# A decoder layer on one core: prompt scores from unsplit queries and keys on the two row halves of the array, and four instead of two channel tiles convolved beside the prompt heads

## The chip, the cores and the metric

One core of a Trainium2 chip runs the whole program. The metric is the device time of one execution in microseconds; of several runs the median counts. Engines are named as the profile names them: PE is TensorE (PEld its weight load), DVE is VectorE, ACT is ScalarE, POOL is GpSimd, SP is SyncE, which here issues DMAs only.

## The reference

One inference step of one layer, for a prompt of 512 tokens and a batch of 8 sample tokens (one each, with 2048 tokens of cached past), all in fp32. D is 1024, there are 16 heads of 64 and 4 groups of keys and values.

```python
z = rms_norm(x, ln1_g) @ w_in            # 6704 columns: u (2048), q, six k/v, head gates, two merge gates
u = u2[..., :D_CONV] * sigmoid(u2[..., D_CONV:])
conv_out = silu(layer_norm(depthwise_conv31(u) + conv_b)) @ w_pw
# attention: three branches (compressed, selected, window), each with its own k and v
s = (q * 64 ** -0.5) @ k.T - slope[head] * (t_q - t_k)      # masked: t_k <= t_q
o = softmax(s) @ v
attn_out = g[0] * o_cmp + g[1] * o_sel + g[2] * o_win       # sigmoid gates per head
m = sigmoid(g_conv) * conv_out + sigmoid(g_attn) * attn_out
x = x + m @ w_out
x = x + square(relu(rms_norm(x, ln2_g) @ w_up)) @ w_down    # 4096 wide
y = rms_norm(x, lnf_g)
```

## The kernel before, in words

**Layout.** All activations lie channel-major: a tile holds 128 channels by 520 tokens (512 of the prompt, 8 samples), and eight tiles make the 1024 channels. Every fp32 matrix product with a weight is made of three reduced-precision (fp32r) ones. The weight is cast to fp32r by ACT (`wh`, L411), the rest `raw - wh` is the low half `wl` (L412), and the activation is split in the same way into `hH` and `hL`. `dense()` adds wh·aH, wh·aL and wl·aH for eight tiles of the inner dimension and two halves of the tokens (L433 to L435): 48 matmuls of some 260 columns for each 128 columns of a weight. `wload()` has SP fetch the raw weight in two pieces. POOL makes the low halves (`LOW[0]`), except those of loads 2 to 5 and of the feed-forward, which DVE makes.

**Stages.** The start is the norm (`norm1()`, L325 ff.), in an order that the string `NORDER` writes out: q squares a tile of tokens on ACT, s takes the statistics of tiles a to b (with a Newton step, L218 to L221, on DVE), m scales a tile (L338), t transposes it on PE and splits it. Then follow two stages in which generators take turns by weights (`run()`); the instructions of each are then placed by a scheduler that goes by priorities, and each engine executes its instructions in the order so found.

The first stage (about 57 to 455 us) holds the prompt's heads. `project()` makes q, k and v of a group, `cmp_kv` the compressed keys, `pool_cache()` gathers and pools the samples' cached rows (L783, L790), and `attend(g)` goes through two pairs of heads, each with three branches: selected (r = 0), window (r = 1), compressed (r = -1). For a branch, a head and a tile of 128 queries there is a score matmul (L688) into one of the two banks of `pss`, a reduction with the distance penalty and the maximum on DVE (`score()`, L651) and an exponential on ACT (L655). After that come the weights, transposes on PE (L750), copies to `pt` (L753), and the product with V (L755), for which the two heads take the two column halves of the array. Beside it `u_proj()` projects the convolution's input u of two channel tiles (`U_EARLY` says behind which score), and `conv_taps()` convolves them: 31 operations on DVE for a channel tile, 30 of them L1108.

For L688 a query tile is split in two (`build_q()`): the rows of head e hold the cast query, the other 64 rows its rest. The key is split in `build_k()` and copied by DMA to both row halves. Two matmuls with all 128 rows, against the cast key and against its rest, then give the score. The tiles of both are called `rt`.

The second stage (to about 725 us) holds the samples' attention, 20 units of a gather of 1 MB (`sg`, issued by POOL), transposes (L936), scores (L940), a reduction (L943), an exponential and the product with V. Beside it run the other six channel tiles (u and taps), the gates `gate_attn()` and `gate_conv()`, and, once all tiles are convolved, the convolution's norm and activation (`conv_norm`, `conv_act`, `conv_split`, L1179 to L1226), which make `cH` and `cL`. Then follow the pointwise product with `merge()`, which takes `cH` as its input, the output projection, the feed-forward and the last norm.

The functions that the change touches:

Of the kernel before, what the change touches and what calls it, by code (L numbers as in the profile page):

```python
# [17 lines left out]
P = 128  # L18
# [15 lines left out]
KTS_B, SG_B, U1, Y1, UP1 = 5, 6, 2, 2, 2  # L34
# [6 lines left out]
LOW2 = "gpsimd"  # L41
# [4 lines left out]
RT_E = lambda nc: nc.gpsimd  # L46
# [6 lines left out]
WR_B, RT_B = 3, 5  # L53
# [3 lines left out]
U_EARLY = (32, 48, 0, 0)  # L57
# [73 lines left out]
def hybrid_layer(ctx: ExitStack, tc: tile.TileContext, I, C, O):  # L131
# [141 lines left out]
    def small_loads():  # L273
        nc.sync.dma_start(wp, I["cmp_w"][0])
# [10 lines left out]
        for i, n in enumerate(("ln2_g", "conv_b", "conv_ln_g", "conv_ln_b")):  # L285
            nc.sync.dma_start(vr[8 * i:8 * i + 8], I[n][0].rearrange("(k p) -> k p", p=P))
        nc.sync.dma_start(cwr, I["conv_w"][0])
# [33 lines left out]
    def norm1():  # L321
# [14 lines left out]
        def scale(j):  # L336
            n = P if j < 4 else NB
            dve.scalar_tensor_tensor(xts[j][:n], xts[j][:n], rs[:n, 0, j:j + 1], g1b[:n], op0=OP.mult, op1=OP.mult)  # L338
# [16 lines left out]
        for op in NORDER.split():  # L355
            a = int(op[1])
            if op[0] == "q":
                squares(a)
            elif op[0] == "s":
                stats(slice(a, int(op[2])))  # L360
            elif op[0] == "m":
                scale(a)
            else:
                last = turn(a)
# [15 lines left out]

    hH = hp.tile([P, KD, T], F32R, name="hH", tag="H")
# [22 lines left out]
    def wload(w, pieces, r0=0, low=None):  # L404
# [46 lines left out]
    ckD = plp.tile([P, NKV, 2, 32], F32R, name="ckD")  # L451
# [16 lines left out]
    def cmp_kv(ap):  # L468
# [49 lines left out]
        for s in range(2):  # L518
            for d in range(2):
                act.activation(ckD[64 * d:64 * d + 64, s:4:2, 0], ps[64 * s:64 * s + 64], AF.Copy, scale=0.5)  # L520
                dve.scalar_tensor_tensor(ckD[64 * d:64 * d + 64, s:4:2, 1], ps[64 * s:64 * s + 64], 0.5,
                                         f32(ckD[64 * d:64 * d + 64, s:4:2, 0]), op0=OP.mult, op1=OP.subtract)
# [32 lines left out]
    def project(g):  # L555
# [4 lines left out]
        kv = kt, vtok = t4[:, 2 * T:3 * T], t4[:, 3 * T:].rearrange("p (t r d) -> p t r d", t=4, r=2)  # L560
# [43 lines left out]
    RT, HP, HV = {}, [], []  # L604

    def build_q(g, pr, ap):
        qc = QC[g]
        t = RT[g, "q", pr] = ap.tile([P, 2, NP_ + 32], F32R, name="rt", bufs=RT_B)
        for e in range(2):
            a, o = 64 * e, 64 - 64 * e  # L610
            act.copy(t[a:a + 64, e, :NP_], qc[a:a + 64, pr, :NP_])
            RT_E(nc).tensor_tensor(t[o:o + 64, e, :NP_], qc[a:a + 64, pr, :NP_], f32(t[a:a + 64, e, :NP_]), op=OP.subtract)

    def build_k(g, r, ap):
        kt = KV[g][0]
        w = ap.tile([P, 2, NP_ + 32], F32R, name="rt", bufs=RT_B)
        t = RT[g, "k", r] = w[:, :, 32:]
        RT[g, "ck", r] = w
        if r == 1 and g > 0:
            add_ck(g)  # L620
        a, o = 64 * r, 64 - 64 * r
        act.copy(t[a:a + 64, 0], kt[a:a + 64, :NP_])
        dve.tensor_sub(t[a:a + 64, 1], kt[a:a + 64, :NP_], f32(t[a:a + 64, 0]))
        DUP_E(nc).dma_start(f32(t[o:o + 64]), f32(t[a:a + 64]))

    def add_ck(g):
        act.copy(RT[g, "ck", 1][:, :, :32], f32(ckD[:, g]))

    def attend(g, ap):
        while g not in QC:  # L630
            yield
        if g == 0:
            build_q(0, 0, ap)
            build_k(0, 0, ap)
            build_k(0, 1, ap)
            build_q(0, 1, ap)
            yield
        elif RT_B < 6:
            build_q(g, 1, ap)
# [1004 lines left out]
```

## Time and profile before

| | |
|---|---|
| median of 3 runs | 1199.09 us (1196.57 to 1199.47) |
| profiled execution, its time | 1196.95 us |
| its span | 1195.2 us |
| mean granted PE clock | 0.981 of full speed |
| PE busy | 1126.9 us (94%) |
| DVE busy | 773.2 us (65%) |
| ACT busy | 557.1 us (47%) |
| POOL busy | 385.2 us (32%) |

All rows are of the one profiled execution, whose span lies 1.75 us below the time of the same execution. Busy shares are means over stages with different limits, so they are read by stage. "out<-in" names the tiles that an instruction writes and reads; what stands behind "<-" in square brackets, or in a wait, is what ended the idle time ahead.

### The profile page before, as it was taken

How to read it: one execution, taken by the hardware profiler on the slowest of the kernel's cores; microseconds unless marked ns; L12 is line 12 of the kernel's file. 1: busy time of each engine (PE TensorE's matmuls, PEld its weight loads, DVE VectorE, ACT ScalarE, POOL GpSimd, SP SyncE). 2: the span in 40 equal slices, each digit the busy share in tenths (PEclk: the TensorE clock that was granted, in tenths of full speed). 3: DMA queues.
4: the chain of work that ended last, by engine and by line, in shares of the span. 5: the costliest groups of instructions: out<-in, count | busy, mean ns of one | idle time of the engine just before them, and what ended most of it. 6: DMA issues, size and time to landing. Idle time of an engine off the chain costs nothing.

```text
span 1195.2 us, 24820 instructions
## 1 busy us (share of the span) xinstructions
PE 1126.9 (94%) x9755; PEld 1025.3 (86%) x9755; DVE 773.2 (65%) x1712; ACT 557.1 (47%) x1404; POOL 385.2 (32%) x378
## 2 busy tenths in 40 slices
PE   6899999998999999989889979999999999999996
PEld 6787976876776888878777769999999999999996
DVE  6442566595977868999998886456543443443476
ACT  5453477545667544445444454344431441431454
POOL 2435637545652333545553334440000000000012
PEclk8899999999999999999999889999999999999999
DMA  6645654564468417867774233333333333333354
GB/s 180 196 137 165 191 168 118 158 175 150 116 185 298 133 38 274 279 241 250 252 253 169 64 105 108 89 89 107 89 96 100 89 89 89 95 99 90 89 164 138
DMA packets 189037, 176.78 MB, mean 148 GB/s; under 512 B 35309, under 2 KB 171053, under 8 KB 183656
## 3 DMA queue, kind: packets, MB, share of 16 engines
q1 hardware_dynamic: 172472, 96.54, 28.5%
q0 software_dynamic: 15296, 76.55, 18.2%
q10 hardware_dynamic: 1152, 2.10, 0.8%
q8 instruction: 77, 1.26, 0.4%
q14 instruction: 40, 0.33, 0.1%
HBM read 167.58 MB, written 14.80 MB: 153 GB/s over the span
## 4 chain that ended last, share of the span: by engine, by line
PE 71%; DVE 20%; DMA 4%; issue 2%; SPq 1%; ACT 1%; POOL 1%; DVEq 0%; POOLq 0%; ACTq 0%
PE psd L433 18%; PE psd L435 17%; PE psd L434 17%; DVE y L1108 13%; PE pss L688 4%; PE pst L750 3%; PE pso L755 3%; PE psp L783 2%; DMA wraw<-in_w_in_dram 1%; DMA cg<-in_cache_cmp_kv_dram,gic 1%; DVE tq L943 1%; DVE y L1212 1%; DMA rt<-rt 1%; PE pso L729 1%; PE psp L790 1%
## 5 line engine op out<-in xcount | busy, mean ns | idle before, releaser
L411 ACT CAST wh<-wraw 128x512 fp32r<-128x512 f32 x282 | 161.7, 617 | 266.9 <-PE psd L434 201.8
L433 PE MATMUL psd<-hH,wh 128*128 128x256 f32 (+2 forms) x848 | 248.3, 295 | 2.2 <-ACT gc L1249 1.3
L435 PE MATMUL psd<-hH,wl 128*128 128x256 f32 (+2 forms) x848 | 247.1, 294 | 0.1
L434 PE MATMUL psd<-hL,wh 128*128 128x256 f32 (+2 forms) x848 | 245.7, 291 | 0.0
L412 POOL TENSOR_TENSOR wl<-wraw,wh 128x512 fp32r<-128x512 f32 x130 | 180.7, 1409 | 199.5 <-ACT wh L411 188.3
L1108 DVE SCALAR_TENSOR_TENSOR y<-u,cwT,y 128x512 f32<-128x512 f32 x240 | 221.7, 924 | 6.0
L433 PEld LDWEIGHTS psd<-hH,wh 128*128 128x128 f32 (+1 forms) x848 | 160.7, 190 | 7.6 <-issue 2.5
L435 PEld LDWEIGHTS psd<-hH,wl 128*128 128x128 f32 (+1 forms) x848 | 160.4, 190 | 4.3 <-issue 2.8
L434 PEld LDWEIGHTS psd<-hL,wh 128*128 128x128 f32 (+1 forms) x848 | 160.8, 190 | 1.8 <-issue 0.7
L433 PE MATMUL psd<-xgH,wh 128*128 128x264 f32 (+1 forms) x512 | 144.8, 283 | 0.0
L434 PE MATMUL psd<-aT,wh 128*128 128x264 f32 (+1 forms) x512 | 144.7, 283 | 0.0
L433 PE MATMUL psd<-aT,wh 128*128 128x264 f32 (+1 forms) x512 | 144.7, 283 | 0.0
L435 PE MATMUL psd<-aT,wl 128*128 128x264 f32 (+1 forms) x512 | 144.7, 283 | 0.0
L435 PE MATMUL psd<-xgH,wl 128*128 128x264 f32 (+1 forms) x512 | 144.5, 282 | 0.0
L412 DVE TENSOR_TENSOR wl<-wraw,wh 128x512 fp32r<-128x512 f32 x152 | 103.9, 723 | 62.5 <-ACT wh L411 59.3
L434 PE MATMUL psd<-xgL,wh 128*128 128x264 f32 (+1 forms) x512 | 144.2, 282 | 0.0
L1583 POOL TENSOR_TENSOR attnT<-attnT,gfb 128x512 f32<-128x512 f32 (+1 forms) x8 | 10.5, 1331 | 368.7 <-DVE sqd L1578 368.7
L434 PEld LDWEIGHTS psd<-xgL,wh 128*128 128x128 f32 x512 | 96.6, 189 | 0.0
L655 ACT ACTIVATE pp<-pp,st 128x256 f32<-128x256 f32 (+3 forms) x128 | 71.6, 559 | 53.7 <-DVE st L651 52.1
L435 PEld LDWEIGHTS psd<-xgH,wl 128*128 128x128 f32 x512 | 96.5, 188 | 0.0
L433 PEld LDWEIGHTS psd<-aT,wh 128*128 128x128 f32 x512 | 96.3, 188 | 0.1
L433 PEld LDWEIGHTS psd<-xgH,wh 128*128 128x128 f32 x512 | 96.3, 188 | 0.0
(378 smaller groups left out, 2326.3 us busy)
## 6 DMA issues: line engine op xcount, KB each, us to landing
wraw<-in_w_in_dram SPq DMA_DIRECT2D x88, 256.0 KB
wraw<-in_w_down_dram SPq DMA_DIRECT2D x80, 256.0 KB
wraw<-in_w_up_dram SPq DMA_DIRECT2D x64, 256.0 KB
sg<-in_state_win_kv_dram POOLq DMA_DIRECT2D x8, 1024.0 KB
out_dram<-in_state_win_kv_dram SPq DMA_DIRECT2D x8, 1022.0 KB
wraw<-in_w_in_dram SPq DMA_DIRECT2D x32, 128.0 KB
wraw<-in_w_conv_pw_dram SPq DMA_DIRECT2D x16, 256.0 KB
wraw<-in_w_out_dram SPq DMA_DIRECT2D x16, 256.0 KB
```

What stands on the lines that cost most here:

```text
L411: act.copy(a, raw[:, :, :o])
L412: (low or (dve if 2 <= len(loaded) < LOW_D else LOW[0])).tensor_tensor(b, raw[:, :, :o], f32(a), op=OP.subtract)
L433: pe.matmul(ps[:n], wh[:, k, :n], aH[:, k, c], start=(k == 0), stop=False)
L434: pe.matmul(ps[:n], wh[:, k, :n], aL[:, k, c], start=False, stop=False)
L435: end = pe.matmul(ps[:n], wl[:, k, :n], aH[:, k, c], start=False, stop=(k == KD - 1))
L655: act.activation(ph, ph, AF.Exp, scale=-1.0, bias=st[:, 0, e, i:i + 1], accum_out=st[:, 1, e, i:i + 1])
L688: hpe = pe.matmul(ps, rq[:, e, P * i:P * i + P], kk[:, l, 32 - xi:32 + nk], start=(l == 0), stop=(l == 1))
L729: packed([lambda i=i, e=e: pe.matmul(po[64 * e:64 * e + 64, P * i:P * i + P], VcZ[:, i], pt[:, e], start=False, stop=True, skip_group_chec ...
L750: pe.transpose(ps[:, o:o + P], phs[e][i][:, P * j:P * j + P], ident)
L755: packed([lambda j=j, e=e: pe.matmul(po[64 * e:64 * e + 64, P * j:], vt[:, j, r], pts[e][:, off[j]:off[j] + P * (4 - j)], start=(r == 0 an ...
L783: packed([lambda r=r, j=j, i=i: pe.matmul(po[32 * i:32 * i + 32, j], wpa[:, 2 * rh + r, j], gs[i][:, r, 256 * j:256 * j + 256], start=(rh ...
L1108: prev = dve.scalar_tensor_tensor(yk, u[:, w:w + NP_], cwT[:, k, w:w + 1], yk, op0=OP.mult, op1=OP.add)
```

## The change

Scores are made in fp32 from the unsplit query and key. A head's query lies in one row half of its tile, so its score needs 64 rows. The key is kept for both row halves: one half as projected, the other as a copy in `ks`. The scores of both heads of a pair are issued together (`packed`), in the steps of query tiles (0, 1), (2) and (3), each head in its own bank; a step waits for the last reduction of both heads. The split tiles `rt` go. The memory lets four channel tiles instead of two have their u and y in the first stage. Low halves from the second stage on are made by DVE, the last two loads and products of the convolution's gate wait for the last sample score, and the start has another order of its norm and of its small loads. The size of a DMA scratch area is now given, 16384.

```diff
-KTS_B, SG_B, U1, Y1, UP1 = 5, 6, 2, 2, 2
+KTS_B, SG_B, U1, Y1, UP1 = 5, 6, 2, 4, 4
-LOW2 = "gpsimd"
+LOW2 = "vector"
-U_EARLY = (32, 48, 0, 0)
+U_EARLY = (32, 48, 56, 74)
-NORDER = "q0 s01 q1 m0 s12 m1 t0 t1 q2 q4 q3 s25 m4 m2 t4 m3 t2 t3"
+NORDER = "q0 q1 s02 m0 m1 t0 t1 q2 q4 q3 s25 m4 m2 t4 m3 t2 t3"
+HELD = 6
     def small_loads():
+        nc.sync.dma_start(cwr, I["conv_w"][0])
+        for i, n in enumerate(("ln2_g", "conv_b", "conv_ln_g", "conv_ln_b")):
+            nc.sync.dma_start(vr[8 * i:8 * i + 8], I[n][0].rearrange("(k p) -> k p", p=P))
...
-    def wload(w, pieces, r0=0, low=None):
+    def wload(w, pieces, r0=0, low=None, ins=None):
...
-            (low or (dve if 2 <= len(loaded) < LOW_D else LOW[0])).tensor_tensor(b, raw[:, :, :o], f32(a), op=OP.subtract)
+            with after(ins):
+                (low or (dve if 2 <= len(loaded) < LOW_D else LOW[0])).tensor_tensor(b, raw[:, :, :o], f32(a), op=OP.subtract)
...
-    ready = [wload(w_in, [(C_Q + P * t, P)]) for t in range(2)]
+    ready = [wload(w_in, [(C_Q + P * t, P)], ins=scaled[1]) for t in range(2)]
...
-    def build_q(g, pr, ap):
...
-    def build_k(g, r, ap):
+    def build_k(g, ap):
+        kw = KV[g][0]
+        ks = ap.tile([P, 32 + NP_], F32, name="ks", bufs=2)
         for e in range(2):
...
+            a, o = slice(64 * e, 64 * e + 64), slice(64 - 64 * e, 128 - 64 * e)
+            KR[g, e, e], KR[g, e, 1 - e] = kw[a], ks[a]
+            if g > 0:
+                DUP_E(nc).dma_start(ks[a, 32:], kw[o, 32:32 + NP_])
+            else:
+                (act.copy if e else dve.tensor_copy)(ks[a, 32:], kw[o, 32:32 + NP_])
...
+            rq = lambda e, i: QC[g][64 * e:64 * e + 64, pr, P * i:P * i + P]
...
-                            for l in range(2):
-                                hpe = pe.matmul(ps, rq[:, e, P * i:P * i + P], kk[:, l, 32 - xi:32 + nk], start=(l == 0),
-                                                stop=(l == 1))
...
+                    for step in ((0, 1), (2,), (3,)):
+                        pb = [pss([P, 512]) for e in range(2)]
...
+                                mms.append(lambda ps=ps, e=e, i=i, xi=xi, nk=nk: pe.matmul(
+                                    ps, rq(e, i), KR[g, e, r][:, 32 - xi:32 + nk], start=True, stop=True))
...
+                        hpe = packed(mms, *last_read.values())
...
     def gate_conv():
         for k in range(KD):
+            while k >= HELD and "scored" not in UY:
+                yield
...
+            dense(wh, wl, hH, hL, lambda hf, c, ps: act.activation(gc[:, c], ps, AF.Tanh, scale=0.5),
+                  ins=UY["scored"] if k >= HELD else None)
```

In the code of the change the lines stand a few lower: L414 is the low half, L679 the score, L739 the transposes, L744 the product with V, L934 the reduction of a sample unit, L1099 the tap.

PE in the middle of the prompt heads, before: scores (L688) stand alone, one head and query tile at a time, among dense matmuls and the pooling of cached rows.

```order
L434 MATMUL psd<-hL,wh 128x264
L688 MATMUL pss<-rt 128x384 x2
L688 MATMUL pss<-rt 128x256 x2
L783 MATMUL psp<-cg,wpa 32x256 x16
L433 MATMUL psd<-hH,wh 128x256
L434 MATMUL psd<-hL,wh 128x256
L435 MATMUL psd<-hH,wl 128x256
L433 MATMUL psd<-hH,wh 128x256
L434 MATMUL psd<-hL,wh 128x256
L688 MATMUL pss<-rt 128x512 x2
```

And now, at a place among the prompt heads:

```order
L744 MATMUL pso<-pt,qkv 64x128 x2
L739 MATMUL pst<-ident,pp 128x128 x3
L679 MATMUL pss<-qkv 128x384
L679 MATMUL pss<-ks,qkv 128x384
L791 MATMUL psp<-pl,w1bd 128x256
L739 MATMUL pst<-ident,pp 128x128 x3
L744 MATMUL pso<-pt,qkv 64x512 x2
L739 MATMUL pst<-ident,pp 128x128 x3
L679 MATMUL pss<-qkv 128x512
L679 MATMUL pss<-ks,qkv 128x512
```

A query tile's scores are now two single matmuls side by side, one from the projected keys (in `qkv`) and one from the copy `ks`. Over the whole stage, PE has 1542 dense matmuls of the input projection ahead of the first sample matmul (its input is `KX`) before, and 1795 in the changed kernel.

DVE near the end of the samples' attention, before (`tq` and `sst` are a unit's biased scores and maximum, `cacc` the sum over channels): the taps go on until the last units, and the norm of the convolution (L1179 ff.) follows them.

```order
L1108 SCALAR_TENSOR_TENSOR y<-u,cwT,y 128x512 x9
L943 ISA tq,sst<-psy,bm 128x512
L943 ISA sst 128x1
L1108 SCALAR_TENSOR_TENSOR y<-u,cwT,y 128x512 x2
L963 COPY a_8136<-sst 32x16 x4
L1080 TENSOR_TENSOR cacc<-cacc,y 128x512
L943 ISA tq,sst<-psy,bm 128x512
L943 ISA sst 128x1
L963 COPY a_8136<-sst 32x16 x4
L1179 TENSOR_TENSOR y<-y,u 128x520 x2
```

And now, where the taps end:

```order
L1099 SCALAR_TENSOR_TENSOR y<-u,cwT,y 128x512 x5
L414 TENSOR_TENSOR wl<-wraw,wh 128x512 x2
L1099 SCALAR_TENSOR_TENSOR y<-u,cwT,y 128x512
L1071 TENSOR_TENSOR cacc<-cacc,y 128x512
L934 ISA tq,sst<-psy,bm 128x512
L934 ISA sst 128x1
L1170 TENSOR_TENSOR y<-y,u 128x520 x8
L414 TENSOR_TENSOR wl<-wraw,wh 128x512 x2
L934 ISA tq,sst<-psy,bm 128x512
L934 ISA sst 128x1
```

Eight of the 20 units' reductions still follow, and the norm's operations now lie between them, with the low halves (L414), which were POOL's. After the heads DVE has 180 taps before and 120 now, and 31 low halves ahead of merge, where it had none.

## Rows read from the trace of the kernel before

**Rows 1.** Stages: columns us, PE, PEld, DVE, ACT, POOL busy (x), PEclk, DMA share, GB/s.

```profile
75.00:450.00 375.00, 361.36 (x2978) 295.76 (x2977) 248.00 (x755) 211.78 (x655) 189.36 (x206) 1.00 0.53 157
450.00:725.00 275.00, 244.94 (x2489) 215.58 (x2489) 249.99 (x392) 133.33 (x290) 117.73 (x103) 0.96 0.60 206
725.00:1195.00 470.00, 460.16 (x3843) 459.14 (x3842) 239.65 (x464) 177.48 (x382) 53.58 (x38) 0.99 0.34 102
```

**Rows 2.** The page's chain that ended last, by engine and by line.

```profile
PE 71%; DVE 20%; DMA 4%; issue 2%; SPq 1%; ACT 1%; POOL 1%; DVEq 0%; POOLq 0%; ACTq 0%
PE psd L433 18%; PE psd L435 17%; PE psd L434 17%; DVE y L1108 13%; PE pss L688 4%; PE pst L750 3%; PE pso L755 3%; PE psp L783 2%; DMA wraw<-in_w_in_dram 1%; DMA cg<-in_cache_cmp_kv_dram,gic 1%; DVE tq L943 1%; DVE y L1212 1%; DMA rt<-rt 1%; PE pso L729 1%; PE psp L790 1%
```

**Rows 3.** Narrower stretches, columns as in rows 1.

```profile
450.00:475.00 25.00, 25.00 (x240) 22.72 (x239) 20.21 (x28) 9.97 (x21) 6.06 (x7) 1.00 0.82 315
450.00:650.00 200.00, 181.41 (x1931) 159.02 (x1931) 190.96 (x258) 95.26 (x216) 96.66 (x88) 0.98 0.73 255
550.00:575.00 25.00, 20.64 (x214) 18.98 (x215) 24.47 (x34) 13.09 (x30) 11.52 (x10) 0.95 0.78 275
700.00:725.00 25.00, 16.70 (x124) 16.20 (x124) 20.90 (x31) 13.26 (x23) 5.59 (x5) 0.86 0.22 64
950.00:975.00 25.00, 25.00 (x211) 25.00 (x210) 12.81 (x26) 12.13 (x28) 0.00 (x0) 1.00 0.29 85
```

**Rows 4.** DVE's timeline at the start; PE's waits from 0 to 75 us.

```profile
7.81 1.28 DVE L338 SCALAR_TENSOR_TENSOR xt<-xt,rs,g1b 128x1024 f32<-128x1024 f32 x1 [0.76 <-DMA g1b<-in_ln_g_dram]
...
9.83 1.03 DVE L218 TENSOR_TENSOR rs<-rs 128x1 f32<-128x1 f32 x1
...
13.34 2.25 DVE L338 SCALAR_TENSOR_TENSOR xt<-xt,rs,g1b 128x1024 f32<-128x1024 f32 x1
...
22.34 0.16 DVE L218 TENSOR_TENSOR rs<-rs 128x3 f32<-128x3 f32 x1
...
PE pss L346 <- DVE xt L338: 5.6, 2, 5.4
...
PE pst L308 <- DMA cwr<-in_conv_w_dram: 2.6, 1, 2.6
```

**Rows 5.** The chain in order of time, 60 to 75 and 100 to 116 us.

```profile
64.91 0.47 PE pss L688 x2
...
103.78 1.01 PE pso L755 x4
...
108.47 0.80 PE pso L755 x4
...
112.36 0.80 PE pso L755 x8
...
113.73 1.06 PE psp L790 x4
```

**Rows 6.** Groups by line and shape, 0 to 460 us, on POOL and DVE.

```profile
L612 POOL TENSOR_TENSOR rt<-qkv,rt 64x512 fp32r<-64x512 f32 x16 | 21.9, 1369 | 29.2 <-DMA cg<-in_cache_cmp_kv_dram,gic 12.0 <-ACT rt L611 7.1 <-DMA bd<-in_cache_cmp_kv_dram,gib 5.2
...
L651 DVE CUSTOM_DVE_ANT_0 pp<-pss,dist 128x512 f32<-128x512 f32 x32 | 22.0, 686 | 11.7 <-PE pss L688 6.2 <-issue 3.0 <-PE pss L697 2.1
```

**Rows 7.** Groups by line, taps from 450 to 725 us, DVE's low halves in the page.

```profile
L1108 DVE SCALAR_TENSOR_TENSOR y<-u,cwT,y 128x512 f32<-128x512 f32 x179 | 165.6, 925 | 5.0
...
L412 DVE TENSOR_TENSOR wl<-wraw,wh 128x512 fp32r<-128x512 f32 x152 | 103.9, 723 | 62.5 <-ACT wh L411 59.3
```

**Rows 8.** Timelines of DVE and of POOL, 470 to 493 us.

```profile
476.44 6.80 DVE L1108 SCALAR_TENSOR_TENSOR y<-u,cwT,y 128x512 f32<-128x512 f32 x5
...
489.60 3.89 DVE L1108 SCALAR_TENSOR_TENSOR y<-u,cwT,y 128x512 f32<-128x512 f32 x5
...
475.31 3.45 POOL L412 TENSOR_TENSOR wl<-wraw,wh 128x512 fp32r<-128x512 f32 x2 [10.73 <-PE psy L940]
```

**Rows 9.** Waits from 450 to 725 us: us in total, times, longest.

```profile
POOL wl L412 <- ACT wh L411: 82.9, 16, 18.6
...
PE psd L433 <- ACT cH L1225: 6.6, 1, 6.6
```

More of the change, by code (lines that the diff above doesn't have):

```diff
@@ L450, in hybrid_layer @@
     pool.memset(gbh, 0.0)
-    ckD = plp.tile([P, NKV, 2, 32], F32R, name="ckD")
+    ckD = plp.tile([P, NKV, 32], F32, name="ckD")
     VcD = plp.tile([P, NKV, HD], F32, name="VcD")
@@ L601, in project @@
             yield
[L604 to L608 removed]
+    KR, HP, HV, last_read = {}, [], [], {}
+    def build_k(g, ap):
+        kw = KV[g][0]
+        ks = ap.tile([P, 32 + NP_], F32, name="ks", bufs=2)
         for e in range(2):
[L610 to L619 removed]
+            a, o = slice(64 * e, 64 * e + 64), slice(64 - 64 * e, 128 - 64 * e)
[4 more added lines that the diff above has]
+                (act.copy if e else dve.tensor_copy)(ks[a, 32:], kw[o, 32:32 + NP_])
+        if g > 0:
             add_ck(g)
[L621 to L624, printed above, removed]
     def add_ck(g):
[L627 removed]
+        for e in range(2):
+            act.copy(KR[g, e, 1][:, :32], ckD[64 * e:64 * e + 64, g])
     def attend(g, ap):
@@ new lines, in attend @@
+                    x = 32 if r == 1 and ride else 0
+                    for step in ((0, 1), (2,), (3,)):
+                        pb = [pss([P, 512]) for e in range(2)]
+                        mms, reads = [], []
+                        for i in step:
+                            nk, xi, o = P * (i + 1), x if i < 3 else 0, P + x if i == 1 else 0
+                            for e in range(2):
+                                ps = pb[e][:, o:o + xi + nk]
+                                mms.append(lambda ps=ps, e=e, i=i, xi=xi, nk=nk: pe.matmul(
+                                    ps, rq(e, i), KR[g, e, r][:, 32 - xi:32 + nk], start=True, stop=True))
+                                reads.append((r, e, i, ps[:, xi:], dbase[:, 384 - P * i:512], phs[e][i], st))
+                                if xi:
+                                    reads.append((-1, e, i, ps[:, :32], dcmp[i], cphs[e][:, i], cst))
+                            for e in range(2) if x and i == 1 else ():
+                                ps = pb[e][:, 448:480]
+                                mms.append(lambda ps=ps, e=e: pe.matmul(ps, rq(e, 3), KR[g, e, r][:, :32], start=True, stop=True))
+                                reads.append((-1, e, 3, ps, dcmp[3], cphs[e][:, 3], cst))
+                        hpe = packed(mms, *last_read.values())
+                        for a in reads:
+                            score(*a)
+                            if a[0] >= 0:
+                                HP.append(hpe)
+                                yield
@@ L703, in attend @@
                         for i in range(4):
-                            for l in range(2):
-                                pe.matmul(psc[:, i], rq[:, e, P * i:P * i + P], ckD[:, g, l], start=(l == 0), stop=(l == 1))
+                            pe.matmul(psc[:, i], rq(e, i), ckD[64 * e:64 * e + 64, g], start=True, stop=True)
                             score(-1, e, i, psc[:, i], dcmp[i], cphs[e][:, i], cst)
@@ L710, in attend @@
                     if r == 0:
-                        build_q(g + 1, 0, ap)
-                        build_k(g + 1, 0, ap)
-                        build_k(g + 1, 1, ap)
-                    elif r == 1 and RT_B > 5:
-                        build_q(g + 1, 1, ap)
+                        build_k(g + 1, ap)
                 while "gates" not in built:
@@ L939, in attend @@
                     yield
-                packed([lambda n=n: pe.matmul(pq[32 * n:32 * n + 32], Qz[:, n % 2, bs[n // 2]], kts[n], start=True, stop=True,
+                run_ = packed([lambda n=n: pe.matmul(pq[32 * n:32 * n + 32], Qz[:, n % 2, bs[n // 2]], kts[n], start=True, stop=True,
                                               skip_group_check=True) for n in range(4)], *cps)
+                if col == SORDER[-1] and e == 1:
+                    UY["scored"] = run_
                 t = sp.tile([P, 512], F32, name="tq", tag="kts", bufs=KTS_B)
@@ L1350, in qk @@
     def qk(name):
-        return qkp.tile([P, 3 * T + NP_], F32, name=name, tag="qk", bufs=QK_B)
+        return qkp.tile([P, 3 * T + 32 + NP_], F32, name=name, tag="qk", bufs=QK_B)
     pa, ap = area("ap")
```

52 lines of the change are left out of this document (13 added, 39 removed).

## The prediction

> **What bounds the kernel now.** I read the table of stages first. TensorE (PE) is busy 361 of 375 us in the stage of the prompt heads (75 to 450) and 460 of 470 us from 725 on, whereas in the stage of the sample attention (450 to 725) it is VectorE (DVE) that is fuller, 250 of 275 us against 245 for PE [rows 1]. The chain of waits agrees: 71% of it is PE, 20% DVE, and the largest DVE line on it, with 13% of the span, is the convolution's tap, L1108 [rows 2]. Narrower stretches show where: DVE is busy for 191 of the 200 us from 450 to 650, at 550 to 575 for 24.47 of 25 us while PE has 20.64, and at 700 to 725 PE is down to 16.70 us [rows 3]. So the kernel is PE-bound, except in the 200 us in which six channel tiles are convolved beside the sample units. A change pays there if it takes work off DVE, and in the other stages only if it takes work off PE.
>
> **Start.** The new order takes the statistics of prompt tiles 0 and 1 in one go. Before, tile 1's own Newton step ran beside the first low halves on POOL: three of its operations took about 1.0 us each (the first 1.03), where the same ones alone took 0.16, and the scaling took 2.25 us against 1.28 [rows 4]. Together that is 3 x 0.87 + 0.97 = 3.6 us, and PE waited 5.4 us for that scaling. With the low halves issued behind the second scaling, and no second step, I take -4 us; waiting for tile 1's squares costs the first tile one activation of about 1 us, which leaves -3. The convolution's weight rows now come first: PE waited 2.6 us for them [rows 4], which goes: -2. **-5 us, between -9 and 0** (nothing, if another load is late in its place).
>
> **Scores.** 128 pairs of split matmuls (K = 128) become 128 fp32 ones (K = 64). A pair of 512 columns took 0.47 us [rows 5]; by columns a head's 1280 of a branch take 1.18 us and the 32 of them 38 us. The chain gives the line 4% of the span, 42 to 54 us [rows 2]. For fp32 the nearest rows are the products of the weights with V (L755), which run two heads in the two column halves: 512 columns of each took 1.01 us, 384 took 0.80, and 256 + 128 took 0.80 [rows 5]. 128 columns more cost 0.21, so 512 cost 0.84 and 0.17 is the group's own. That the halves do run together shows against L790, which uses one part of the array: four records of 256 columns took 1.06 us, four of 512 columns in L755 took 1.01. A branch of two heads is the same three groups, 2.61 us; there are 16 such branches (4 groups, 2 pairs of heads, 2 branches): 41.8 us. Against 38 to 54 for the old form I put **0 us, -12 to +4**. No row has row halves; their bound is one half after the other: 2 x (2.61 - 0.51) + 0.51 = 4.71 us a branch, 16 x 2.1 = +34 us. I take the price of the column halves, because both forms are fp32 products on disjoint cells of the array, and the order puts the two heads' products of a step on PE one behind the other.
>
> The Trainium skill, page "TensorE: Matmul & The Clock Gate" (Part 3, the table of packed matmuls), gives four row tiles of K = 32 only 3.07 times the rate of one. If two halves are as far from their ideal, an estimate from that figure is 2 x 2.1 / 1.53 + 0.51 = 3.25 us a branch, which would add 10 us and make the sum -13 in place of -23; the column halves in this trace show no such loss.
>
> **Splitting.** The split of queries and keys goes: 16 casts of queries on ACT, 16 subtractions on POOL (21.9 us), and the casts of keys [rows 6]. In their place come six copies by DMA and two on ACT and DVE for the first group. PE was busy 361 of 375 us in the stage, so none of this was on the path: **0 us**. It frees some 22 us of POOL, which nothing here waits for.
>
> **Two more channel tiles early.** With the projections of four channels' u among the heads, the order of PE holds 253 more dense matmuls ahead of the first sample product (1542 before, 1795 now). One took 25.00 / 211 = 0.119 us where PE ran full [rows 3]: +30 us to a stage that had 13.6 us of PE idle [rows 1]. Four more blocks of work to draw on fill a little of that, say 2 us: **+28 us, 25 to 36** (the upper end if heads and loads get in each other's way). The 60 extra taps that come along fit on DVE: 248 + 56 = 304 of some 400 us, so they cost nothing as long as PE bounds the stage.
>
> **The sample stage.** DVE loses the taps: after the heads it had 180, now 120, so 60 x 0.925 = -55 us [rows 7]. Its other 119 get quicker, since POOL no longer subtracts low halves: five taps while POOL subtracted took 6.80 us, five others 3.89, that is 1.36 and 0.78 each [rows 8]; 119 x (0.925 - 0.78) = -17. It gains 31 low halves at 0.72 us: +22 [rows 7]. So DVE comes to 250 - 55 - 17 + 22 = 200 us. PE comes to 245 - 30 = 215 us and is the bound again; with about 10 us of gaps (it had 30 while DVE was full, and 14 in the stage before) it needs 225 to 230. From 450 to 650 the DMA engines were busy for 0.73 of the time, 0.82 in the best slice [rows 3], most of it gathers of the sample caches: 146 us at the least for these 200, so about 152 is about as short as they get. I take -44 for these 200 us and -2 for the end of the stage, where two gates of the convolution are now held back to give PE work after the last score: **-46 us, -62 to -20**. What is late next is PE, with dense matmuls, and behind it the gathers. At the end, the wait of 6.6 us of merge's first matmul for the convolution's last activation [rows 9] should go, as DVE's order now has the normalisation done ahead of the last score.
>
> **Later stages.** Low halves on DVE in merge and the output projection: PE is busy 460 of 470 us there and DVE 240 [rows 1]. **0 us**; without that cover 0.72 a half.
>
> **Sum.** -5 + 0 + 0 + 28 - 46 + 0 = -23 us. The profiled execution took 1196.95 us (span 1195.2), which makes 1174; the median of the runs is 2.1 us above it, so I say **1176 us**.
>
> **Rivals.**
> A. *Row halves one after the other.* Then the change does not do what it says: -23 + 34 = +11, 1210 us. For it: no row shows two row halves at once. Against: the column halves, which do overlap. Chance 0.07.
> B. *Low halves stand in DVE's queue (slower).* POOL waited 82.9 us, 16 times, 18.6 at the longest, for ACT's casts, which wait for weights or a free buffer [rows 9]. POOL had nothing else to do; on DVE taps and score reductions stand behind each wait. At half of it, 41 us, DVE needs 200 + 41 + its present 25 of gaps = 266, the stage shrinks by 9 and the sum is -5 + 28 - 9 = +14: 1213 us. It decides from 28 us of standing on: 200 + 28 + 25 = 253, a shrink of 22, and with the 28 and the start nothing is gained. Against: the order places the low halves among taps that are themselves late. Chance 0.13.
> C. *PE waits for both banks.* A step of two heads needs both score banks free, where one was enough. If each of 48 steps waits for one whole reduction (0.69 us [rows 6]), that is 33 us, the sum +10, 1209 us; at half of it the time lies within the forecast's range. Against: dense matmuls, transposes and pooling stand between steps. Chance 0.07.
> D. *The gathers set the stage.* If DMA holds at its best slice, 0.82, the 200 us can shrink to 146 / 0.82 = 178, by 22, with 2 at the end: -5 + 28 - 24 = -1, 1198 us. For it: the gathers already keep it at 0.73, and weights come between. Against: slices are paced by DVE, which frees the buffers. Chance 0.15.
>
> **How the numbers follow.** The forecast has 0.58; its own range is 1152 to 1196, from the ends of its terms taken partly together. A measurement of this kernel can tell 0.3%, 3.6 us, from no change. Faster: 0.56 of the forecast and 0.08 of D, 0.64. Same: 0.02 of the forecast, 0.07 of D, 0.02 of C, 0.11. Slower: A, B and 0.05 of C, 0.25. For 8 in 10 the range takes in the forecast, D, and the milder forms of B and C, and leaves out A and some 0.13 of B and C: 1150 to 1206.
>
> **What would show it.** The table of stages: the first score of the sample attention some 23 us later, merge's first matmul some 23 us earlier. The scores' groups at about 1.0, 0.8 and 0.8 us on the chain, with 1.85 and above for A. Taps after the heads near 0.78 us and 120 of them; DVE under 22 of 25 us beside the sample units, PE above 23. For B: DVE idle ahead of low halves, released by ACT's casts, by 28 us or more. For C: PE waits before the scores, released by DVE. For D: DMA above 0.8 with PE and DVE both idle. The prediction is wrong if the sample stage shrinks by less than the prompt stage grows.

## The result, and the profile after

The changed kernel takes 1188.90 us in the median of 5 runs (1185.94 to 1196.35); the kernel before, on the same chip, 1196.57 (1195.43 to 1199.47). The ratio is 0.9929 [0.9906, 0.9952], a gain of 8.5 us, 0.7%. I had said 1176, a gain of 23. The sign held and the time lies in the range, but the size was out by more than a factor of two.

The profiled execution happens to be the longest of its five, 1196.35 us, so the kernel was profiled once more (the first run below: 1187.36 us, 0.9923 [0.9894, 0.9951]). First the page's chain of the changed kernel, by engine and by line:

```profile
PE 73%; DVE 13%; DMA 8%; issue 2%; ACT 2%; POOL 1%; SPq 1%; DVEq 0%; ACTq 0%; POOLq 0%
PE psd L435 18%; PE psd L436 18%; PE psd L437 18%; DVE y L1099 5%; DMA wraw<-in_w_in_dram 3%; PE psx L925 3%; PE psp L772 3%; DMA sg<-in_cache_slc_kv_dram,gix 2%; PE pss L679 2%; DMA cg<-in_cache_cmp_kv_dram,gic 2%; PE pso L744 2%; PE pst L739 2%; DVE pp L643 2%; DVE pp L728 2%; PE psy L941 2%
```

Against [rows 2] DVE falls from 20% to 13%, the tap from 13% to 5%, the scores (now L679) from 4% to 2%. In its place stand waits for DMA, 8% against 4%: gathered cache tiles (`sg`) and weights. The shift from DVE that the prediction described took place. It had named the gathers as what is late behind PE, and as rival D; the sum gave them nothing.

Where the time went is read best by two marks on PE: the first sample product, which ends the prompt stage, and merge's first matmul, which ends the sample stage. The table of stretches, columns as in [rows 1], is cut at these marks (0 to the first, the first to the second) and, in a third row, from the first to the last transpose of a gathered tile: the 20 sample units. The kernel before:

```profile
0.00:454.80 454.80, 426.60 (x3471) 354.96 (x3471) 285.77 (x861) 247.51 (x736) 216.03 (x242) 0.98 0.55 163
454.80:710.30 255.50, 227.14 (x2351) 198.51 (x2350) 236.04 (x370) 123.15 (x273) 113.76 (x97) 0.97 0.62 210
460.30:653.90 193.60, 175.01 (x1851) 153.11 (x1850) 188.45 (x260) 95.10 (x217) 92.04 (x82) 0.98 0.70 242
```

The changed kernel, first profile, then second:

```profile
0.00:503.30 503.30, 469.01 (x3724) 368.21 (x3724) 337.02 (x946) 242.50 (x739) 190.66 (x222) 0.97 0.52 153
503.30:710.20 206.90, 193.07 (x2099) 166.07 (x2098) 157.70 (x324) 115.67 (x251) 49.44 (x52) 0.98 0.69 237
```

```profile
0.00:491.80 491.80, 463.94 (x3725) 366.63 (x3725) 332.17 (x946) 243.04 (x739) 191.24 (x222) 0.98 0.52 157
491.80:699.00 207.20, 192.35 (x2098) 165.74 (x2097) 157.62 (x324) 115.28 (x251) 50.30 (x52) 0.98 0.68 236
497.30:674.80 177.50, 164.26 (x1766) 141.99 (x1765) 138.78 (x250) 107.62 (x235) 50.30 (x52) 0.99 0.73 252
```

In the second profile the prompt stage ends 37.0 us later (491.8 against 454.8; forecast +23), the sample stage is 48.3 us shorter (207.2 against 255.5; forecast -46), and the rest changes by less than 1 us: -12 us by span, 2 to 3 more than by the medians, as this execution lies 2.4 us below the median of its six. The first profile has the same sample stage, 206.9 us, and a prompt stage longer by 11.5 us with the same work in it: 5.1 of them are PE's busy time, at a granted clock of 0.97 against 0.98, the other 6.4 idle time. So the sample stage came out as forecast, and the prompt stage grew by 14 us more. But the third rows show that even the right figure had the wrong make-up: the units went from 193.6 to 177.5 us, by 16 where I had 44, and what lies behind their last transpose, up to merge, from 56.4 to 24.2, by 32 where I had 2. DVE's busy time in the stage fell from 236.0 to 157.6 us, further than forecast (250 to 200): 100 taps are left in it, not 120.

The experiments follow with their edits. Times are ratios to the kernel before on the same chip.

### The profile page after: what moved, and what is told of

Read it like the earlier page. It is cut to its first block, busy times and chain, and to the rows that moved or that the text cites. A ratio compares the mean times of both kernels' runs of the same rounds, so it can differ in the third digit from the quotient of the medians.

```text
span 1194.5 us, 24755 instructions
## 1 busy us (share of the span) xinstructions
PE 1135.8 (95%) x9755; PEld 1006.2 (84%) x9755; DVE 747.4 (63%) x1773; ACT 542.6 (45%) x1384; POOL 253.0 (21%) x284
## 4 chain that ended last, share of the span: by engine, by line
PE 73%; DVE 13%; DMA 8%; issue 2%; ACT 2%; POOL 1%; SPq 1%; DVEq 0%; ACTq 0%; POOLq 0%
PE psd L435 18%; PE psd L436 18%; PE psd L437 18%; DVE y L1099 5%; DMA wraw<-in_w_in_dram 3%; PE psx L925 3%; PE psp L772 3%; DMA sg<-in_cache_slc_kv_dram,gix 2%; PE pss L679 2%; DMA cg<-in_cache_cmp_kv_dram,gic 2%; PE pso L744 2%; PE pst L739 2%; DVE pp L643 2%; DVE pp L728 2%; PE psy L941 2%
## 5 line engine op out<-in xcount | busy, mean ns | idle before, releaser
L435 PE MATMUL psd<-hH,wh 128*128 128x264 f32 (+2 forms) x848 | 249.9, 296 | 4.4 <-ACT hH L348 2.2
L437 PE MATMUL psd<-hH,wl 128*128 128x264 f32 (+2 forms) x848 | 245.7, 292 | 0.2 <-POOL wl L414 0.2
L436 PE MATMUL psd<-hL,wh 128*128 128x264 f32 (+2 forms) x848 | 245.0, 290 | 0.4 <-DVE hL L349 0.4
L414 DVE TENSOR_TENSOR wl<-wraw,wh 128x512 fp32r<-128x512 f32 (+1 forms) x230 | 154.5, 707 | 77.5 <-ACT wh L412 73.2
L1099 DVE SCALAR_TENSOR_TENSOR y<-u,cwT,y 128x512 f32<-128x512 f32 x240 | 192.7, 803 | 4.5
L435 PEld LDWEIGHTS psd<-hH,wh 128*128 128x128 f32 (+1 forms) x848 | 160.5, 190 | 13.5 <-issue 7.1
L435 PEld LDWEIGHTS psd<-aT,wh 128*128 128x128 f32 x512 | 96.3, 188 | 0.1
L436 PEld LDWEIGHTS psd<-aT,wh 128*128 128x128 f32 x512 | 96.2, 188 | 0.0
```

Source lines behind the costliest of these rows:

```text
L435: pe.matmul(ps[:n], wh[:, k, :n], aH[:, k, c], start=(k == 0), stop=False)
L436: pe.matmul(ps[:n], wh[:, k, :n], aL[:, k, c], start=False, stop=False)
L437: end = pe.matmul(ps[:n], wl[:, k, :n], aH[:, k, c], start=False, stop=(k == KD - 1))
L1099: prev = dve.scalar_tensor_tensor(yk, u[:, w:w + NP_], cwT[:, k, w:w + 1], yk, op0=OP.mult, op1=OP.add)
```

## Experiments

**Again, and two or three tiles.** The first run is the changed kernel; the next two have fewer channel tiles early.

```diff
-KTS_B, SG_B, U1, Y1, UP1 = 5, 6, 2, 4, 4
-U_EARLY = (32, 48, 56, 74)
+KTS_B, SG_B, U1, Y1, UP1 = 5, 6, 2, 2, 2
+U_EARLY = (32, 48, 0, 0)
```

(with three: 3, 3 and 32, 48, 56, 0.)

> The changed kernel itself, for a second profile. Its profiled execution lay at 1196.4 us where the median of its runs is 1188.9. If the lateness of the first sample product (503.3 us, 48.5 us later than before) belongs to the change, it is again 43 to 50 us later and the sample stage (first sample product to merge's first matmul, 206.9 us) stands near 207. If the profiled execution was merely a poor one, the first sample product lies near 480 (25 later) and the time below 1188. Time by the first: 1186 to 1192.

> Only two channel tiles early, all else as changed; PE has 1517 dense matmuls ahead of the first sample product. Theory 1 (the 76 taps that moved into the prompt stage stand on DVE ahead of the heads' score reductions and make it longer): the first sample product falls back to 445 to 452 us, that is by 278 x 0.119 = 33 us for the matmuls and some 15 to 20 more for the taps; the time is 1186 to 1194, as the sample stage is DVE's again. Rival 2 (the packed scores, which need both banks, lengthen the stage): the first sample product stays at 465 us or later, and the time is 1205 or more.

> Three channel tiles early; 1608 dense matmuls ahead of the first sample product. Theory 1: between the two, first sample product at 462 to 475 us; the time is 1180 to 1188, a little below the changed kernel, as DVE is full in neither stage. Rival 2: first sample product at 480 or later, time 1195 or more.

Measured: 0.9923 [0.9894, 0.9951], two 0.9874 [0.9846, 0.9902] (1181.49 us), three 0.9846 [0.9818, 0.9874] (1176.95 us). With two tiles:

```profile
0.00:456.30 456.30, 430.28 (x3447) 330.39 (x3448) 267.42 (x853) 229.25 (x710) 174.38 (x212) 0.99 0.55 167
456.30:700.20 243.90, 232.03 (x2417) 205.56 (x2416) 219.84 (x416) 129.84 (x284) 52.54 (x54) 0.98 0.63 212
457.40:634.30 176.90, 174.80 (x1878) 154.27 (x1877) 166.66 (x279) 100.00 (x224) 52.54 (x54) 1.00 0.74 255
```

With three:

```profile
0.00:471.40 471.40, 442.07 (x3537) 343.46 (x3537) 305.04 (x903) 233.71 (x719) 181.42 (x217) 0.99 0.52 158
471.40:693.60 222.20, 214.61 (x2302) 189.68 (x2301) 193.17 (x378) 128.72 (x280) 48.95 (x53) 0.98 0.67 232
478.30:658.70 180.40, 176.95 (x1895) 156.25 (x1894) 155.91 (x270) 105.67 (x235) 48.95 (x53) 1.00 0.75 256
```

From two to four tiles the prompt stage grows by 35.5 us; the 278 dense matmuls more make 278 x 0.119 = 33 of it. Theory 1's extra for taps is 2 us, not 15 to 20, so it falls as a reason of its own; rival 2 falls too, as the stage with two tiles ends at 456.3. The taps do stand on the chain of the prompt stage now (12.2% of it, 3.2% before), and DVE is busy for 49.9 of the 50 us from 400 to 450; but PE's idle time in the stage is 27.9 us with four tiles and 26.0 with two, so this costs at most some 2 us. The mark itself scatters: four profiles with the same 1795 dense matmuls ahead of it (the changed kernel's two, and the two gather variants of it below) have it at 490.8 to 503.3, and the second profile's 491.8 lies between the 497.8 to 504.8 and the 480 that I had set out. The times with two and three tiles came out below what either theory gave. The sample stage gives back 36.7. That is the same work moved from one stage in which PE is full to another: with two tiles PE is busy 174.8 of the units' 176.9 us. Four tiles are 0.5% slower than two by the ratios, whose intervals just touch. Three beat both kernels clear of noise; that they beat two (0.9846 against 0.9874) is within the intervals.

**Low halves.** In the changed kernel back to POOL, and in the kernel before on DVE.

```diff
-LOW2 = "vector"
+LOW2 = "gpsimd"
```

> Low halves of the later stages on POOL again. By my prediction they cost DVE 22 us and give back 17 in quicker taps, while PE bounds the sample stage: the time within 4 us of the changed kernel. If the quicker taps are what shortened the sample stage: its taps go back from 0.77 to about 0.92 us, the stage grows from 207 to 215 to 222 us, and the time is 1197 or more. If low halves on DVE delay the stage (rival B): it gets shorter by 5 us or more.

> The kernel before with one edit: the low halves of the later stages on DVE. Theory 1 (low halves on POOL slow the taps, and moving them is most of the change's gain, as their return cost the changed kernel 21 us): 1174 to 1182 us; taps of the sample stage near 0.80 in place of 0.92 us, the stage 235 to 240 in place of 255.5 us, the prompt stage as before. By the terms of my prediction DVE, which bounds the stage, gains 26 and loses 22: 1191 to 1195. If low halves stand in DVE's queue (rival B): above 1199.

Measured: on POOL 1.0111 [1.0079, 1.0142], that is 1.9% above the changed kernel; in the kernel before, on DVE, 0.9987 [0.9964, 1.0010], nothing that can be told, and neither theory 1's 1174 to 1182 us nor the 1191 to 1195 of my terms (1197.37). DVE's groups in the sample stage, of the kernel before with low halves on DVE, of the changed kernel, and of that with low halves on POOL:

```profile
L1108 DVE SCALAR_TENSOR_TENSOR y<-u,cwT,y 128x512 f32<-128x512 f32 x178 | 136.5, 767 | 4.1
L412 DVE TENSOR_TENSOR wl<-wraw,wh 128x512 fp32r<-128x512 f32 x44 | 30.7, 706 | 19.1 <-ACT wh L411 19.1
```

```profile
L1099 DVE SCALAR_TENSOR_TENSOR y<-u,cwT,y 128x512 f32<-128x512 f32 x100 | 76.5, 765 | 2.2
L414 DVE TENSOR_TENSOR wl<-wraw,wh 128x512 fp32r<-128x512 f32 x31 | 20.7, 685 | 11.5 <-ACT wh L412 11.4
```

```profile
L1099 DVE SCALAR_TENSOR_TENSOR y<-u,cwT,y 128x512 f32<-128x512 f32 x96 | 83.6, 871 | 2.4
```

The taps quicken as forecast: 0.767 us with low halves on DVE, against 0.925 [rows 7]; the 31 halves cost 20.7 us (forecast 22). DVE stands idle ahead of them for ACT's casts for 11.4 us, where rival B decides from 28 on. The quicker taps alone don't explain 21 us in one kernel and 2 in the other, as DVE is not full in the changed kernel's units (138.8 of 177.5 us). POOL's waits differ more, with low halves on POOL and then in the changed kernel:

```profile
POOL wl L414 <- ACT wh L412: 62.5, 14, 14.4
...
POOL sg L317 <- PE psy L941: 18.7, 6, 5.9
```

```profile
POOL sg L317 <- PE psy L941: 62.8, 12, 7.9
```

POOL issues the gathers. With low halves in its queue it waits 62.5 us for casts and only 18.7 for free gather buffers; without them, 62.8 for buffers, and the next gather goes out as soon as one is free. My line that POOL "had nothing else to do" was wrong. What this queue costs was argued, not shown. The sample stage with low halves on POOL:

```profile
498.00:717.70 219.70, 198.90 (x2112) 168.53 (x2111) 157.96 (x290) 116.11 (x253) 95.46 (x83) 0.97 0.66 230
```

By span the difference is 23 us: 12.5 in this stage (219.7 against 207.2), 6 in the prompt stage, within the scatter of its end, and 4 behind, in merge. Of the 12.5, PE's idle time makes 6 (20.8 against 14.9) and its busy time 6.5, with some 13 matmuls more and a granted clock of 0.97 against 0.98. And PE's waits for gathered tiles are not longer, 6.0 us against 9.1. So gathers that go out later can be only a part of it; the rest stays open. In the kernel before the units shorten from 193.6 to 183.5 us with this edit (first transpose 468.2, last 651.7), but they begin 13.5 us behind the first sample product in place of 5.5, and the stretch behind them grows from 56.4 to 62.6. The late start has its own cause, shown at the end of this section.

**Start and held gates.** The changed start on top of that kernel; the changed kernel with the old order of the norm and no wait for the second scaling; two and three tiles without the hold (`HELD = 8`). The edit of the second:

```diff
-NORDER = "q0 q1 s02 m0 m1 t0 t1 q2 q4 q3 s25 m4 m2 t4 m3 t2 t3"
+NORDER = "q0 s01 q1 m0 s12 m1 t0 t1 q2 q4 q3 s25 m4 m2 t4 m3 t2 t3"
-    ready = [wload(w_in, [(C_Q + P * t, P)], ins=scaled[1]) for t in range(2)]
+    ready = [wload(w_in, [(C_Q + P * t, P)]) for t in range(2)]
```

> The same with the changed start as well (order of the norm, small loads, low halves behind the second scaling). If the first dense matmul's 3.3 us are carried to the end: 2 to 5 us below the one without. If the wait for the weight rows has only moved to the next small load: 0 to 3 below.

> The changed kernel with the old order of the norm and low halves that do not wait for the second scaling (small loads as changed). If the start is worth what the first dense matmul shows (3.3 us): 1189 to 1192. If it is lost again before the first sample product, as the two kernels before with and without it suggest: within 2 us of the changed kernel. By my prediction 3 us slower.

> Three channel tiles early, and the last two gates of the convolution not held back for the last score. If holding gives PE work it lacked (my term of 2 us): 1 to 5 us slower than with it, 1178 to 1182. If it delays merge, whose first weights wait behind it: 2 to 6 us faster, 1171 to 1175.

> Two channel tiles early, and no gates held back. If holding is worth something only where dense work runs out before the last score: 5 to 12 us slower than with it, 0.993 to 0.997. If it is worth nothing, as with three tiles: 0.986 to 0.989, and the sample stage within 3 us of 243.9.

Measured: 0.9958 [0.9936, 0.9980] with the start, against 0.9987 without; 0.9939 [0.9921, 0.9958] with the old start, against 0.9923. Both point to 2 to 4 us, with intervals that overlap. Without the hold three tiles take 0.9840 [0.9809, 0.9871] against 0.9846, two 0.9864 [0.9832, 0.9896] against 0.9874: the hold is worth nothing that can be told. PE's waits up to 75 us in the changed kernel:

```profile
PE pst L346 <- DVE xt L338: 2.1, 1, 2.1
PE pst L300 <- DMA pos<-in_cmp_pos_dram: 1.7, 1, 1.7
...
PE pss L346 <- DVE xt L338: 0.3, 1, 0.3
```

The wait for the scaling fell from 5.6 us [rows 4] to 2.4, and the wait for `cwr` went. The next small load, `pos`, took its place: 1.7 us here, 3.2 in the first profile, 3.6 to 3.9 in the variants with two and three tiles.

**The step of two heads.** The wait for the last reductions of both heads is taken out of the order; each matmul still waits for its own bank.

```diff
-                        hpe = packed(mms, *last_read.values())
+                        hpe = packed(mms, )
```

> The changed kernel without the order that a step of scores waits for the last reduction of both heads; each head's matmul still waits until its own bank is free. If that wait is what lengthens the prompt stage beyond its matmuls (rival C): first sample product at 480 to 485 us in place of 491.8 (with 21 dense matmuls more ahead of it, 2.5 us), the time 1178 to 1182. If it costs nothing: 490 to 496 us and 1185 to 1192. If it keeps the two heads in step: their matmuls no longer start together and the scores cost up to 34 us more.

Measured: 1.0215 [1.0182, 1.0249], 1224.87 us; the first sample product comes at 523.3 us. The timeline of PE around two heads' products of 512 columns, without the wait and in the changed kernel:

```profile
210.14 1.12 PE L679 MATMUL pss<-ks,qkv 64*128 64x512 f32 x2
...
211.78 1.12 PE L679 MATMUL pss<-qkv 64*128 64x512 f32 x2
```

```profile
313.81 0.67 PE L679 MATMUL pss<-ks,qkv 64*128 64x512 f32 x1 [0.28 <-DVE st L643]
313.82 0.69 PE L679 MATMUL pss<-qkv 64*128 64x512 f32 x1
314.32 0.59 PE L679 MATMUL pss<-ks,qkv 64*128 64x512 f32 x1
314.35 0.59 PE L679 MATMUL pss<-qkv 64*128 64x512 f32 x1
314.87 0.39 PE L437 MATMUL psd<-hH,wl 128*128 128x256 f32 x1
```

With the wait, the two heads' products begin 0.01 us apart, the last ends 1.13 us after the first start (314.35 + 0.59 - 313.81), and PE's next matmul starts after 1.06. Without it, the two heads' products stand apart in PE's order: one runs alone, for 1.12 us, and after other work the other's. The stage grows by 31.5 us, 2.5 of them for 21 matmuls more ahead of the mark. PE's busy time in the score matmuls (L679; columns us, PE busy, clock, DMA share, GB/s), with the wait and without it; then all of the stage without it; then PE's wait for the reductions in the changed kernel:

```profile
0.00:491.80 491.80, 49.65 (x256) 0.98 0.52 157
0.00:523.30 523.30, 88.80 (x256) 0.99 0.49 147
...
0.00:523.30 523.30, 507.52 (x3745) 384.15 (x3745) 341.77 (x950) 246.71 (x740) 188.07 (x222) 0.99 0.49 147
...
PE pss L679 <- DVE st L643: 3.1, 3, 1.7
```

The same 256 matmuls keep PE busy for 39 us more, while its idle time in the stage falls by 12 (27.9 to 15.8). So the wait of rival C is what prevents rival A. By this its price is some 12 us at the most, 3.1 of them direct waits for the reductions, where the rival had 33.

**Gathers.** Half of the gathers of the selected cache are left out in both kernels: the second unit of a column uses the tiles of the first. And five gather buffers in place of six, in the changed kernel.

```diff
-                    g = self.cached(b, 2 * e + i) if col < NB else self.window(b)
+                    if col < NB and e == 1:
+                        g = keep[i]
+                    else:
+                        g = self.cached(b, 2 * e + i) if col < NB else self.window(b)
+                        keep[i] = g
```

```diff
-KTS_B, SG_B, U1, Y1, UP1 = 5, 6, 2, 4, 4
+KTS_B, SG_B, U1, Y1, UP1 = 5, 5, 2, 4, 4
```

> The changed kernel with half the gathers of the selected cache: the second unit of a column reuses the tiles of the first, so it attends to the wrong heads' rows; all compute stays. If the gathers pace the sample units now (rival D; the 178 us from first to last transpose in which PE is busy 165): the units take 165 to 170 us and the time is 1174 to 1180, 8 to 13 us less. If PE's own waits on its products pace them: 0 to 3 us less.

> The kernel before with the same halved gathers, whose units take 194 us with DVE busy 189. If DVE paced them, as the prediction reads it: within 4 us of the kernel before. If the gathers did so there already: 10 us or more below.

> The changed kernel with five buffers for gathered tiles in place of six. If the gathers pace the units by the turn of their buffers: up to 178 x 6 / 5 = 214 us for the units, 15 to 36 us slower, 1202 to 1223. If DMA's rate paces them, or PE: within 6 us, up to 1194.

Measured: half the gathers 0.9876 [0.9847, 0.9904], half in the kernel before 0.9924 [0.9902, 0.9946], five buffers 1.0210 [1.0173, 1.0247]. The sample stage and the units with half the gathers, then with five buffers:

```profile
490.80:691.00 200.20, 189.91 (x2098) 163.46 (x2097) 161.70 (x332) 119.28 (x260) 33.73 (x36) 0.99 0.49 163
496.40:660.50 164.10, 162.11 (x1761) 140.10 (x1760) 136.11 (x247) 104.70 (x229) 33.73 (x36) 1.00 0.51 167
```

```profile
496.30:738.40 242.10, 203.29 (x2099) 167.29 (x2098) 161.19 (x331) 121.02 (x259) 51.31 (x53) 0.95 0.59 208
501.80:709.80 208.00, 175.06 (x1767) 143.70 (x1766) 139.69 (x252) 110.21 (x236) 51.31 (x53) 0.95 0.62 218
```

With half the gathers PE is full again, 162.1 of 164.1 us, and the units take 13.4 us less; the whole gains 6 us, less than the 8 to 13 that I expected, since the stretch behind them, up to merge, grows. The changed kernel's, then with half the gathers:

```profile
674.80:699.00 24.20, 22.59 (x266) 18.30 (x264) 13.69 (x66) 6.90 (x16) 0.00 (x0) 0.95 0.28 89
660.50:691.00 30.50, 22.20 (x270) 17.83 (x268) 20.38 (x77) 13.76 (x31) 0.00 (x0) 0.93 0.32 96
```

PE has the same work there and 6.7 us more of idle time. With five buffers the units take 208 us, near 177.5 x 6 / 5 = 213, at a DMA share of 0.62; 10.8 of the 30.5 us more are PE's busy time on the same matmuls, at a granted clock of 0.95 against 0.99, the rest idle time. So it is the turn of the buffers (product with V, issue, transfer, transposes) that paces the units in the changed kernel, not DMA's rate; rival D had the right place and the wrong limit. The kernel before gained 9 us from half the gathers where I expected under 4. Its units shorten by only 4 us (first transpose 459.4, last 649.2), so that DVE paced them in the main, as I read it; another 2.2 us come in merge (its matmuls by `cH` span 50.9 us in place of 53.1), and the rest is spread.

**All but scores and tiles.** The kernel before with low halves on DVE, the start and the hold. The edits are those of the change; the size of the scratch area stays as before.

> The kernel before with low halves on DVE, the changed start and the held gates: all of the change but the scores and the two channel tiles. It differs from the variant with two channel tiles (1181.5 us, 0.9874) by the form of the scores alone. If the scores' form is worth nothing in itself, as my prediction has it: 0.985 to 0.990, so that holding the gates is what the 10 us between that variant and the kernel before with low halves and start come from. If the form of the scores brings them: 0.994 to 0.998, and the sample stage near 258 us.

Measured: 0.9953 [0.9934, 0.9973]. Its stretches:

```profile
0.00:457.10 457.10, 429.51 (x3467) 357.89 (x3468) 284.61 (x867) 247.25 (x734) 197.16 (x228) 0.97 0.54 164
457.10:716.60 259.50, 234.37 (x2397) 206.68 (x2396) 221.06 (x413) 128.76 (x281) 50.92 (x54) 0.95 0.62 211
470.70:653.30 182.60, 175.25 (x1860) 154.10 (x1858) 168.36 (x277) 98.45 (x220) 50.92 (x54) 0.98 0.70 241
```

The variant with two tiles differs from it by the scores and by the given size of the scratch area, which was not tried by itself: 0.9874, 0.8% less. No difference can be told in the prompt stage (457.1 and 456.3 us, with 20 dense matmuls fewer in the latter). The sample stage differs by 15.6 us, more than the 0.8% (9.5 us); this execution is the longest of its twelve, 1199.12 us against a median of 1194.48. PE's idle time in the stage makes 13.3 of them (25.1 against 11.9). The first unit comes late: the first transpose stands at 470.7, 13.6 us behind the first sample product, and at 457.4, 1.1 behind it, with the new scores. ACT's timeline, and the waits from 445 to 475 us:

```profile
456.99 0.62 ACT L413 CAST wh<-wraw 128x512 fp32r<-128x512 f32 x1 [2.29 <-PE psd L437]
466.90 0.62 ACT L413 CAST wh<-wraw 128x512 fp32r<-128x512 f32 x1 [9.29 <-DMA wraw<-in_w_in_dram]
```

```profile
DVE wl L415 <- ACT wh L413: 12.2, 3, 9.0
ACT wh L413 <- DMA wraw<-in_w_in_dram: 9.3, 1, 9.3
...
PE psd L436 <- ACT ah L1064: 6.3, 1, 6.3
```

A weight arrives late at the border of the stages; its cast and its low half on DVE stand 9 us, and PE waits. That is 6.3 of the 13.3 us; 5.3 are in the units and 1.7 behind them. It is no chance of one profile: with the old scores and low halves on DVE all three kernels here have it (the first transpose 13.5 to 13.7 us behind the mark, ACT's wait for the weight 9.2 to 9.3), and with the old scores and low halves on POOL, 5.5 us, it isn't there. This is rival B's mechanism, once, in kernels that aren't the change. With the new scores' order the load is not late. Why the order of loads comes out differently there was not tried.

## Why the prediction was wrong, point by point

**The step that failed** is the pair of terms for the two channel tiles: +28 in the prompt stage, and most of the -46 in the sample stage. I took DVE to bound the sample stage as long as six tiles are convolved in it, so that moving two of them out would pay more there than it cost in the prompt stage. But with the rest of the change and six tiles in it PE is already full (174.8 of the units' 176.9 us). From two to four tiles the runs show +35.5 us in the one stage and -36.7 in the other, and a time that is 0.5% longer. The gain comes from the other parts of the change: with two tiles early they give 1.3% (0.9874), where the sum had little more than the start's -5 us.

**What bounds the kernel** was right for the kernel before: PE, and DVE beside the sample units, where its taps fell from 13% to 5% of the chain of waits.

**Start, -5 us**, came out smaller. The wait for the scaling shrank as reckoned, but the wait for a small load only passed to the next one, the case that I had put at the end of the range. The pairs of runs point to 2 to 4 us. The end of the prompt stage does not tell: with the new start it came 2.0 us later in the one pair (456.7 against 454.7) and 3.6 earlier in the other (491.8 against 495.4), both within the scatter of this mark.

**Scores, 0 us.** The price of the group was near right: 1.06 us for 512 columns against 1.01, and 49.7 us of PE for all of L679 against 41.8. Row halves run together like column halves. Rival A's price, +34, was also near what the run without the common wait lost: 39 us of PE in L679, 31.5 in the stage. My estimate from the figure for four row tiles on the Trainium skill's page "TensorE: Matmul & The Clock Gate" (Part 3), which would have added 10 us, is not borne out for two halves: the two take 1.13 us together from first start to last end, one alone 1.12. In the prompt stage no worth of the form can be told. About half of the idle time behind its 0.8% lies at the border, which no term had; the other half is spread, and its cause is open.

**Splitting, 0 us.** One piece of it was on the path after all: "DMA rt<-rt" has 1% of the chain [rows 2], and PE waited 3.0 us for the first copy. In its place PE waits 0.9 us for `qkv` (3.9 in the first profile), so the term stays near nothing.

**Two more channel tiles, +28 us.** From two to four tiles PE had 278 matmuls more ahead of the mark (253 is the difference to the kernel before), and the stage grew by 35.5 us: nothing of them was absorbed by idle time, where I had 2 us. For 253 that is 32, inside the term's range. The stage as a whole grew by 37 in place of +23: some 4 are this term, up to 7 the start, and the rest lies within the scatter of the mark.

**The sample stage, -46 us**, came out at -48.3 by two errors that cancel, which is luck: -16 in place of -44 in the units, -32 in place of -2 behind them. I charged the gain to DVE's missing taps. But with the other parts of the change, two tiles already leave PE full in the units, so what four tiles took out of that stage, 36.7 us, was PE's own 33 us of matmuls. They only changed places, and the stretch after the units shrank. And fewer matmuls did not shorten the units: they take 176.9 us with two tiles, 180.4 with three, 177.5 with four (175.4 with the old start), while PE's share falls from 99% to 93%. With two and three tiles PE is nearly full; with four it is the turn of the six gather buffers that holds them, as five buffers and half the gathers show.

**Sum.** Taken in the order of the runs, low halves give 0.1%, the start 0.3%, the hold 0.05%, the scores 0.8%, and the tiles cost 0.5%: 0.7 to 0.8%. Of these only the scores' share is clear of the intervals, and in another order the shares differ: in the changed kernel the low halves are worth 1.9%. I had the tiles as the gain, and of the rest the start alone. The cuts of the stages could have shown it: PE stood at 245 of 275 us in the stage that was to be relieved [rows 1]. By the stretches above, PE's idle time goes from 28.4 to 14.9 us in the sample stage (255.5 - 227.1, 207.2 - 192.3) and stays at 28 in the prompt stage (28.2 and 27.9), while its busy time in both grows by 2.6: that is the whole gain of 11.3 us up to merge. I had 16 us of idle time closing in the sample stage (46 less the 30 of matmuls), 2 in the prompt stage, and the start's 5 on top.

**Later stages, 0 us**: with low halves on POOL merge takes 4 us longer (its matmuls by `cH` span 56.6 us against 52.3), so there too it is no loss to have them on DVE.

## What to carry to other kernels

Work moved between two stages with the same bound is worth only the idle time that it closes; count that engine's idle time in both stages before and after the move, and try the smaller move too, since the best may lie between (three tiles here, 1.5% under the kernel before, with four at 0.8%). An engine that seems idle may issue transfers: look at what stands in its queue ahead of them (POOL waited 62.5 us for casts there), though what that cost was not shown here. And a wait that keeps two halves of the array in step can be worth more than its price: 39 us of PE against 12 at the most.

## What was not expected of the hardware

Two products of 64 rows on the two row halves, into different banks, begin 0.01 us apart and are through in 1.13 us for 512 fp32 columns, where one alone takes 1.12. And one kernel's prompt stage differed by 11.5 us between two executions (503.3 and 491.8), with equal matmuls and gathers and the same stage behind it; the mean granted clock was 0.97 and 0.98, which goes with less than half of it. So the end of a stage in one profile is not to be read to a few us.
